# Working out the experts' order, and loading it into registers, before the first gather instead of after the first expert's first group

## The chip, the cores and the metric

The kernel runs on one core of a Trainium2 chip. A time is the device time in microseconds (us) of one execution; three were taken of the kernel before. The engines have short names in the profile: PE is TensorE (matmuls), PEld its weight loads, DVE is VectorE, ACT is ScalarE, POOL is GpSimd, SP is SyncE, which here issues nearly all transfers; SPq is SyncE's instruction queue. Each engine carries out its own list of instructions in order, and waits at an instruction until the semaphores that it names are there.

## The reference

Two layers run over 256 tokens of 1024 features (and over 256 context tokens in the first layer). The second layer ends in a mixture of 8 experts, and all that the change touches lies there: the router gives every token 8 scores, the best two count, and each expert is a gated two-layer network of width 3584.

```python
def moe_swiglu(h, router, w1, w3, w2):
    logits = (h @ router).astype(jnp.float32)
    vals, idx = lax.top_k(logits, TOP_K)          # TOP_K = 2
    wts = jax.nn.softmax(vals, axis=-1)
    combine = jnp.sum(jax.nn.one_hot(idx, N_EXPERTS) * wts[..., None], axis=-2)
    y = jnp.zeros_like(h)
    for e in range(N_EXPERTS):                    # 8 experts
        y = y + combine[..., e:e + 1] * swiglu(h, w1[e], w3[e], w2[e])
    return y
# swiglu(h, w1, w3, w2) = (silu(h @ w1) * (h @ w3)) @ w2
```

## The kernel before, in words

**Experts by rank.** An expert is not computed for all tokens. Its tokens are gathered by a matmul with a one-hot matrix into a block of 128 columns ("large") or 64 columns ("small"). Expert 0 is always large and always first. The other seven are sorted by their number of tokens while the kernel runs: the three fullest are large, the four others small. Which expert stands at which rank is known only on the chip, so SyncE loads the seven expert numbers into registers, and the address of a weight transfer is taken from a register. `SEQ` is the fixed order of the blocks: expert 0, then small and large in turn.

**The steps.** The list `steps` holds the whole kernel. A step is a function and the weight tiles that it needs; a tile is 1024 KB. An expert's 3584 hidden features are cut into seven f-groups of 512. An f-group takes six tiles: two each of `moe1` and `moe3` (the two input matrices, `eh` for large and `eh_small` for small) and two of `moe2` (the output matrix, `ey`, `ey_small`), which is computed one block later. `seq` is the list of (block, f-group): (0,0), (0,1), (1,0), (0,2), and so on, a large and a small one in turn. So the first ten tiles, those of (0,0) and (0,1) and of the output of (0,0), belong to expert 0 and have fixed addresses; the eleventh is the first of a small block and needs the registers. Here they are called tile 1 to tile 10, and tile 11 onwards.

**The path of a tile.** `issue_dma` puts the transfers on SyncE's queue in the order of the steps, as far as buffers are free: five called `raw` and five called `q`. It stops at `state["stop"]`, the first tile with an address from a register, until `order_load` lifts the stop. For a large block a tile is split: ScalarE casts it to a high part (`hi`, line 233), VectorE subtracts (`lo`, line 211), and TensorE runs three matmuls (lines 261 to 263) for each product; there are three `hi` and three `lo` buffers, and VectorE's subtraction frees the transfer's buffer. For a small block the tile is used as it came (line 1536), and the matmul frees the buffer. `ensure` writes the split of a tile into the program two tiles ahead of its step, so that the splits stand between the other instructions of ScalarE and VectorE.

**Around the change.** `route_b` chooses the two experts of each token, and sums by matmul the rank of each token within its expert (`rank`) and the number of tokens of each expert (into columns 16 to 24 of the same PSUM tile). It normalises the tokens in eight feature slices (line 1331 on VectorE, 1333 on ScalarE), transposes them into `htok` (line 1343 on TensorE), and gathers expert 0's tokens (`gather(0)`, line 1478); then it works out the weights of the two experts (`comb`) and copies the counts (`cnt`). `order_a` turns the counts into ranks (`rk`) and the expert numbers by rank (`exi`). `order_load` loads these into SyncE's registers and lifts the stop. `order_b` sorts the columns of `sel`, `comb` and `rank` by rank (`by`), and works out whether any block overflows (`cmi`, read at the very end). `onehots_small` makes the one-hots of the four small blocks, and `gather_small` gathers all four at once (line 1491 on TensorE, copied by ScalarE at line 1492). Where each is called stands in the loop at the end of the listing.

Of the kernel before, what the change touches and what calls it, by code (L numbers as in the profile page):

```python
# [22 lines left out]
F32 = mybir.dt.float32  # L23
# [8 lines left out]
P = 128  # L32
# [6 lines left out]
E = 8  # L39
# [47 lines left out]
def build(ctx, tc, io):  # L87
    nc = tc.nc
    ve, se, te = nc.vector, nc.scalar, nc.tensor
# [150 lines left out]
    def step(fn, *gs, native=False, quiet=False, late=False):  # L240


        steps.append(([(g, native) for g in gs], fn, quiet, late))
# [1053 lines left out]
    def route_b(_):  # L1297
        pb = C["ss"].bcast()
        r = C["ss"].r
        iota8 = iota[:, :E]  # L1300
        sel = cp.tile([P, 2, E], F32, name="sel")
        comb = cp.tile([P, 2, E], F32, name="comb")
        rank = cp.tile([P, 2, E], F32, name="rank")
        lgs = tiny(16).rearrange("p (t e) -> p t e", t=2)
        mx = tiny(16).rearrange("p (t e) -> p t e", t=2)
        ix = tiny(16, U32).rearrange("p (t e) -> p t e", t=2)
        for t in range(2):
            ve.scalar_tensor_tensor(lgs[:, t, :], C["lg"][t][:, :E], r[:, t:t + 1], C["c0"], op0=ALU.mult, op1=ALU.add)
            ve.max(mx[:, t, :], lgs[:, t, :])
            ve.max_index(ix[:, t, :], mx[:, t, :], lgs[:, t, :])  # L1310
        del C["lg"]
        xf = tiny(4).rearrange("p (t c) -> p t c", t=2)
        ve.tensor_copy(xf, ix[:, :, 0:2])
        o0 = tiny(16).rearrange("p (t e) -> p t e", t=2)
        o1 = tiny(16).rearrange("p (t e) -> p t e", t=2)
        for t in range(2):
            ve.tensor_scalar(o0[:, t, :], iota8, xf[:, t, 0:1], None, op0=ALU.is_equal)
            ve.tensor_scalar(o1[:, t, :], iota8, xf[:, t, 1:2], None, op0=ALU.is_equal)
        ve.tensor_add(sel, o0, o1)
        tri = cst[:, K_TRI:K_TRI + P]  # L1320
        ps = PS()
        te.matmul(ps[:, 0:E], lhsT=tri, rhs=sel[:, 0, :], start=True, stop=True)
        te.matmul(ps[:, E:2 * E], lhsT=tri, rhs=sel[:, 1, :], start=True, stop=False)
        te.matmul(ps[:, E:2 * E], lhsT=ones, rhs=sel[:, 0, :], start=False, stop=True)
        te.matmul(ps[:, 2 * E:3 * E], lhsT=ones, rhs=sel[:, 0, :], start=True, stop=False)
        te.matmul(ps[:, 2 * E:3 * E], lhsT=ones, rhs=sel[:, 1, :], start=False, stop=True)

        hn = []
        for k in range(KD):
            t = S()  # L1330
            ve.tensor_mul(t[:, :L], xt[k][:, :L], pb[:, :L])
            hn.append(xt[k][:, L:])
            se.activation(hn[k], t[:, :L], AF.Identity, bias=mod(1, SH2 + k, 0), scale=Affn[1][:, k, 0:1])
            if k == 3:
                ve.tensor_copy(rank, ps[:, 0:2 * E].rearrange("p (t e) -> p t e", t=2))
                C["sel"], C["comb"], C["rank"] = sel, comb, rank
                onehots(0)
        htok = C["htok"] = pools["t"].tile([P, 2, D], F32, tag="htok", name="htok")
        for hf in range(2):
            for t in range(2):  # L1340
                pt = PS()
                for k in range(4):
                    te.transpose(pt[:, k * P:(k + 1) * P], hn[4 * hf + k][:, t * P:(t + 1) * P], ident)
                (se.copy if t else ve.tensor_copy)(htok[:, t, hf * 512:(hf + 1) * 512], pt)
        gather(0)
        flush_tails()

        w = tiny(6).rearrange("p (c t) -> p c t", t=2)
        ve.tensor_sub(w[:, 0, :], mx[:, :, 1], mx[:, :, 0])
        se.activation(w[:, 0, :], w[:, 0, :], AF.Exp)  # L1350
        ve.tensor_scalar(w[:, 1, :], w[:, 0, :], 1.0, None, op0=ALU.add)
        ve.reciprocal(w[:, 1, :], w[:, 1, :])
        ve.tensor_mul(w[:, 2, :], w[:, 0, :], w[:, 1, :])
        for t in range(2):
            ve.tensor_scalar(o0[:, t, :], o0[:, t, :], w[:, 1, t:t + 1], None, op0=ALU.mult)
            ve.scalar_tensor_tensor(comb[:, t, :], o1[:, t, :], w[:, 2, t:t + 1], o0[:, t, :], op0=ALU.mult, op1=ALU.add)
        cnt = C["cnt"] = cp.tile([P, E], F32, name="cnt")
        ve.tensor_copy(cnt, ps[:, 2 * E:3 * E])


    SEQ = ((1, None), (0, 3), (1, 0), (0, 4), (1, 1), (0, 5), (1, 2), (0, 6))
    NR7, LARGE, SMALL = E - 1, 3, 64

    def order_a(_):

        cnt, i7 = C["cnt"], iota[:, :NR7]
        key = tiny(E)
        ve.scalar_tensor_tensor(key, cnt, float(E), iota[:, :E], op0=ALU.mult, op1=ALU.subtract)
        C["ord"] = S()[:, :4 * NR7 * NR7].rearrange("p (i c) -> p i c", i=4)
        m2 = [C["ord"][:, i, :].rearrange("p (a b) -> p a b", a=NR7) for i in range(4)]  # L1370
        k7 = key[:, 1:]
        ve.tensor_tensor(m2[0], k7.unsqueeze(1).broadcast_to([P, NR7, NR7]), k7.unsqueeze(2).broadcast_to([P, NR7, NR7]),
                         op=ALU.is_gt)
        rk = C["rk"] = cp.tile([P, NR7], F32, name="rk")
        ve.reduce_sum(rk, m2[0], axis=AX.X)
        ve.tensor_tensor(m2[1], rk.unsqueeze(1).broadcast_to([P, NR7, NR7]), i7.unsqueeze(2).broadcast_to([P, NR7, NR7]),
                         op=ALU.is_equal)
        ve.tensor_tensor(m2[2], m2[1], iota[:, 1:E].unsqueeze(1).broadcast_to([P, NR7, NR7]), op=ALU.mult)
        ex = tiny(NR7)
        ve.reduce_sum(ex, m2[2], axis=AX.X)  # L1380
        C["exi"] = cp.tile([P, NR7], I32, name="exi")
        ve.tensor_copy(C["exi"], ex)
# [21 lines left out]
        C["cmi"] = cp.tile([P, 1], I32, name="cmi")  # L1404
        ve.tensor_copy(C["cmi"], cmx)

    def order_load(_):

        _, C["ex"] = nc.values_load_multi_w_load_instructions(
            C["exi"][0:1, :], engines=[mybir.EngineType.SP], min_val=1, max_val=E - 1)  # L1410
        state["stop"] = None
        issue_dma()
# [227 lines left out]
    for i, (n, fg) in enumerate(seq):  # L1640
        prev, before = (seq[i - 1] if i else None), (seq[i - 2] if i > 1 else None)
        for part in range(2):
            if SEQ[n][0]:
                for half in range(2):
                    step(eh(n, fg, part, half), expert("moe3" if part else "moe1", n, fg, half))
            else:
                step(eh_small(n, fg, part), expert("moe1", n, fg, part), expert("moe3", n, fg, part), native=True)
            if prev and part == 0:
                step(lambda g, prev=prev: et(*prev))
        if prev:  # L1650
            for half in range(2):
                y_step(*prev, half)
        if before and before[1] == last:
            step(lambda g, m=before[0]: scatter(m))
        if i == 0:
            step(order_a)
            step(order_load)
        if i == 1:
            step(order_b)
            step(onehots_small)  # L1660
            step(gather_small)
        if fg == 3:
            step(lambda g, n=n: comb_t(n))
# [239 lines left out]
```

## Time and profile before

| | |
|---|---|
| time, median of 3 runs | 1897.54 us (1897.12 to 1899.59) |
| the profiled execution's own time | 1896.34 us |
| its span, first to last instruction | 1894.6 us |
| mean granted TensorE clock | 0.981 of 2.4 GHz |
| busy in the span: PE, DVE, ACT, POOL | 95%, 60%, 41%, 23% |
| moved by DMA | 489.99 MB, mean 259 GB/s |
| transfers of expert weights | 334 of 1024.0 KB, the last tiles in halves |

The experts' stage begins near 990 us and goes on to the end. The shares are means over stages with different limits, so the rows below come from the stretch where the change lies (980 to 1060 us), and from two stretches further on. A row with a window gives, for each engine, the busy time in us within that window; "PEclk" is the clock that was granted, and the share of the DMA engines goes up to about 1.

### The profile page before, as it was taken

The page shows a single profiled execution, that of the slowest core. Times are in us where ns is not written, and L with a number is a line of the kernel's source. Part 1 is how long each engine was busy: PE and PEld are TensorE (multiplying, and loading weights), DVE is VectorE, ACT ScalarE, POOL GpSimd, SP SyncE. Part 2 cuts the span into 40 slices and gives each one's busy share as a digit, 9 for nine tenths or more (in the row PEclk, how much of TensorE's full clock was granted, in tenths as well). Part 3 has the DMA queues.
Part 4 walks back from the last instruction along what each step waited for, and adds up shares of the span by engine and source line. Part 5 has one row for each costly group of instructions (what it writes and reads, how often), then busy time and mean ns, then how long its engine had stood idle before and what let it go on. Part 6 is the DMA issues. An engine that isn't in the chain of part 4 may idle for free.

```text
span 1894.6 us, 24116 instructions
## 1 busy us (share of the span) xinstructions
PE 1792.9 (95%) x9438; PEld 1304.5 (69%) x9438; DVE 1137.6 (60%) x1645; ACT 772.5 (41%) x867; POOL 443.5 (23%) x189
## 2 busy tenths in 40 slices
PE   6999999999999999988995999999999999999997
PEld 5889878788888888786584665656556665656563
DVE  5888873398897321768756345555555655555553
ACT  5455542522222222255634344444444444444441
POOL 1677545254444444426400000000000000000000
PEclk9999999999999999999997999999999999999999
DMA  9432153544444322420075799999999999999995
GB/s 369 161 132 90 67 199 138 197 159 175 171 159 159 119 103 89 159 108 23 21 291 222 293 419 419 417 368 410 420 420 393 399 413 420 409 376 406 419 420 213
DMA packets 71686, 489.99 MB, mean 259 GB/s; under 512 B 8080, under 2 KB 9488, under 8 KB 13200
## 3 DMA queue, kind: packets, MB, share of 16 engines
q1 hardware_dynamic: 70992, 487.88, 64.9%
q8 instruction: 76, 1.25, 0.3%
q10 hardware_dynamic: 576, 0.52, 0.1%
q14 instruction: 42, 0.34, 0.1%
HBM read 487.32 MB, written 1.05 MB: 258 GB/s over the span
## 4 chain that ended last, share of the span: by engine, by line
PE 68%; DMA 13%; DVE 11%; ACT 4%; issue 3%; SPq 0%; POOL 0%; DVEq 0%; ACTq 0%; POOLq 0%
PE p L261 17%; PE p L263 17%; PE p L262 17%; DMA raw<-in_moe 11%; PE p L1536 8%; DVE lo L211 3%; ACT hi L233 2%; PE p L1593 2%; PE p L1161 2%; DMA q<-in_moe 2%; DVE p L568 1%; PE p L1556 1%; PE p L370 1%; PE p L1143 1%; DVE s L299 1%
## 5 line engine op out<-in xcount | busy, mean ns | idle before, releaser
L211 POOL TENSOR_TENSOR lo<-raw,hi 128x2048 fp32r<-128x2048 f32 (+1 forms) x69 | 314.7, 4564 | 422.0 <-ACT hi L233 415.2
L233 ACT CAST hi<-raw 128x2048 fp32r<-128x2048 f32 x173 | 329.5, 1908 | 187.0 <-PE p L263 78.3
L261 PE MATMUL p<-s,hi 128*128 128x512 f32 x960 | 375.7, 391 | 0.7 <-ACT s L433 0.7
L262 PE MATMUL p<-s,hi 128*128 128x512 f32 x960 | 374.8, 390 | 1.5 <-DVE s L763 1.1
L263 PE MATMUL p<-s,lo 128*128 128x512 f32 x960 | 374.2, 390 | 0.6 <-POOL lo L205 0.6
L211 DVE TENSOR_TENSOR lo<-raw,hi 128x2048 fp32r<-128x2048 f32 (+1 forms) x108 | 247.0, 2289 | 87.2 <-ACT hi L233 87.2
L211 DVE TENSOR_TENSOR lo<-q,hi 128x2048 fp32r<-128x2048 f32 x69 | 158.0, 2292 | 222.0 <-ACT hi L233 222.0
L233 ACT CAST hi<-q 128x2048 fp32r<-128x2048 f32 x69 | 131.4, 1906 | 197.3 <-DMA q<-in_moe 149.7
L262 PEld LDWEIGHTS p<-s,hi 128*128 128x128 f32 x960 | 180.6, 188 | 40.2 <-DVE s L763 1.7
L261 PEld LDWEIGHTS p<-s,hi 128*128 128x128 f32 x960 | 180.7, 188 | 39.7 <-ACT s L433 0.9
L263 PEld LDWEIGHTS p<-s,lo 128*128 128x128 f32 x960 | 180.6, 188 | 38.6 <-POOL lo L205 1.1
L263 PE MATMUL p<-hi,xg 128*128 128x512 f32 x448 | 175.4, 391 | 5.4 <-DVE xg L1482 5.4
L261 PE MATMUL p<-hi,xg 128*128 128x512 f32 x448 | 179.3, 400 | 0.0
L262 PE MATMUL p<-lo,xg 128*128 128x512 f32 x448 | 175.6, 392 | 0.3 <-DVE lo L211 0.2
L262 PE MATMUL p<-lo,s 128*128 128x256 f32 (+1 forms) x480 | 161.3, 336 | 5.9 <-POOL lo L211 3.9
L261 PE MATMUL p<-hi,s 128*128 128x256 f32 (+1 forms) x480 | 164.7, 343 | 0.0
L396 DVE SCALAR_TENSOR_TENSOR s<-raw,o 128x512 f32<-128x512 f32 x128 | 158.8, 1302 | 0.0
L1536 PE MATMUL p<-q,xt 128*64 128x512 f32 x560 | 156.3, 611 | 0.0
L445 DVE SCALAR_TENSOR_TENSOR xt<-p,mod,xt 128x256 f32<-128x256 f32 x216 | 90.3, 476 | 76.9 <-PE p L263 69.5
L568 DVE SCALAR_TENSOR_TENSOR p<-s,vecs,p 128x494 f32<-128x494 f32 (+11 forms) x192 | 125.9, 736 | 6.1 <-ACT p L550 6.1
L263 PE MATMUL p<-hi,s 128*128 128x512 f32 (+1 forms) x352 | 123.6, 351 | 0.0
L261 PEld LDWEIGHTS p<-hi,s 128*128 128x128 f32 x480 | 92.4, 192 | 30.2 <-issue 21.9
(252 smaller groups left out, 2225.0 us busy)
## 6 DMA issues: line engine op xcount, KB each, us to landing
raw<-in_moe SPq DMA_DIRECT2D x181, 1024.0 KB, 10.3
q<-in_moe SPq DMA_DIRECT2D x153, 1024.0 KB, 13.9
raw<-in_ff SPq DMA_DIRECT2D x42, 1024.0 KB, 4.8
raw<-in_ada SPq DMA_DIRECT2D x31, 1024.0 KB, 5.8
raw<-in_adaT SPq DMA_DIRECT2D x16, 1024.0 KB, 4.9
raw<-in_w_ag SPq DMA_DIRECT2D x8, 1024.0 KB, 6.9
raw<-in_w_uv SPq DMA_DIRECT2D x8, 1024.0 KB, 4.9
raw<-in_w_out SPq DMA_DIRECT2D x6, 1024.0 KB, 5.0
```

Source lines behind the costliest of these rows:

```text
L211: eng.tensor_sub(lo[:, sl], r[:, sl], f32(hi[:, sl]))
L233: se.copy(hi, raws[i])
L261: te.matmul(out, lhsT=lh[0], rhs=rh[0], start=first, stop=False, skip_group_check=True)
L262: te.matmul(out, lhsT=lh[0], rhs=rh[1], start=False, stop=False, skip_group_check=True)
L263: te.matmul(out, lhsT=lh[1], rhs=rh[0], start=False, stop=last, skip_group_check=True)
L299: ve.tensor_add(self.acc[:, :n], self.acc[:, :n], q[:, :n])
L396: ve.scalar_tensor_tensor(j, g[0][:, jj * D + q * 512:jj * D + (q + 1) * 512], 1.0, C["cb"][s][q], op0=ALU.mult, op1=ALU.mult, accum_out=h ...
L445: ve.scalar_tensor_tensor(xt[d][:, sl], ps[:, sl], mod(l, gbase + d, s), xt[d][:, sl], op0=ALU.mult, op1=ALU.add)
L568: ve.scalar_tensor_tensor(ov[:, :, lo:hi], gv[:, :, lo + s:hi + s], vecs[:, w0 + j:w0 + j + 1], ov[:, :, lo:hi], op0=ALU.mult, op1=ALU.add)
L1161: te.matmul(ps[HD * z:HD * z + HD, :L], lhsT=v, rhs=t[:, z, c, :], start=(c == 0), stop=(c == 3), skip_group_check=True, tile_position=(0, ...
L1536: te.matmul(ps[SMALL * z:SMALL * (z + 1), :], lhsT=xt[k][:, o:o + SMALL], rhs=w[z][:, kk, :], start=(k == 0), stop=(k == 7), skip_group_ch ...
L1593: te.matmul(yps[n][SMALL * z:SMALL * (z + 1), :], lhsT=hT[:, f * SMALL:(f + 1) * SMALL], rhs=w[:, ff, z * 512:(z + 1) * 512], start=(fg == ...
```

## The change

Four things are moved; nothing is computed anew and nothing is left out.

- The copy of the counts, `order_a` and `order_load` go from behind the first block's step into `route_b`, between the fourth and the fifth of the eight feature slices, right behind the one-hots of expert 0. They are called there directly and are no steps any more.
- `order_b` goes from behind the second block's last step to a step behind the first half of (0,0).
- `onehots_small` goes from the same place to a step behind the second half of (0,0).
- `gather_small` stays where it was.

```diff
@@ route_b
                 C["sel"], C["comb"], C["rank"] = sel, comb, rank
                 onehots(0)
+                cnt = C["cnt"] = cp.tile([P, E], F32, name="cnt")
+                ve.tensor_copy(cnt, ps[:, 2 * E:3 * E])
+                order_a()
+                order_load()
...
-        cnt = C["cnt"] = cp.tile([P, E], F32, name="cnt")
-        ve.tensor_copy(cnt, ps[:, 2 * E:3 * E])
...
-    def order_a(_):
+    def order_a():
...
-    def order_load(_):
+    def order_load():
@@ the loop over seq
             if prev and part == 0:
                 step(lambda g, prev=prev: et(*prev))
+            if i == 0:
+                step(onehots_small if part else order_b)
...
-        if i == 0:
-            step(order_a)
-            step(order_load)
         if i == 1:
-            step(order_b)
-            step(onehots_small)
             step(gather_small)
```

In the rows of the program's order a line number, an operation, the output and the inputs stand in a row, and a number behind a name tells buffers apart. On VectorE, in `route_b`, this stood behind the one-hots of expert 0 (lines 1331 and 1344 are the normalised slices and the copies of the transposed tokens):

```order
L1426 TENSOR_SCALAR s_8232<-cst,rank,sel 128x128 x2
L1331 TENSOR_TENSOR s_8235<-xt_84,p_8190 128x256
L1331 TENSOR_TENSOR s_8238<-xt_85,p_8190 128x256
L1331 TENSOR_TENSOR s_8241<-xt_86,p_8190 128x256
L1331 TENSOR_TENSOR s_8244<-xt_87,p_8190 128x256
L1344 COPY htok<-p_8248 128x512
```

and this stands there now, where the lines after the change are two or four higher:

```order
L1428 TENSOR_SCALAR s_8232<-cst,rank,sel 128x128 x2
L1339 COPY cnt<-p_8213 128x8
L1370 SCALAR_TENSOR_TENSOR t_8237<-cnt,cst 128x8
L1374 TENSOR_TENSOR s_8239<-t_8237 128x49
L1377 TENSOR_REDUCE rk<-s_8239 128x7
L1378 TENSOR_TENSOR s_8239<-rk,cst 128x49
L1380 TENSOR_TENSOR s_8239<-s_8239,cst 128x49
L1382 TENSOR_REDUCE t_8245<-s_8239 128x7
L1384 CAST exi<-t_8245 128x7
L1331 TENSOR_TENSOR s_8317<-xt_84,p_8190 128x256
```

Eight small instructions now stand ahead of the fifth slice. Further on in VectorE's list, the small blocks' one-hots (line 1436) stood behind the subtractions of tiles 15, 16 and 17 (`q_8467` to `q_8471`) and behind `order_b`, whose last row is `cmi`:

```order
L211 TENSOR_TENSOR lo_8554<-q_8467,hi_8553 128x2048
L211 TENSOR_TENSOR lo_8572<-q_8469,hi_8571 128x2048
L211 TENSOR_TENSOR lo_8588<-q_8471,hi_8587 128x2048
L1392 TENSOR_TENSOR s_8385<-s_8385,sel 128x49
L1393 TENSOR_REDUCE by_8591<-s_8385 128x7
...
L1405 CAST cmi<-t_8612 128x1
L1436 TENSOR_SCALAR s_8617<-cst,by_8601,by_8591 128x64 x8
```

and now they stand among the subtractions of expert 0's own tiles (`q_7819` is tile 5, `raw_7884` tile 6, `raw_7952` tile 7, `raw_8103` tile 8), with `order_b` ahead of tile 6:

```order
L211 TENSOR_TENSOR lo_8428<-q_7819,hi_8427 128x2048
L1394 TENSOR_TENSOR s_8239<-s_8239,sel 128x49
...
L1407 CAST cmi<-t_8454 128x1
L211 TENSOR_TENSOR lo_8473<-raw_7884,hi_8472 128x2048
L1523 TENSOR_TENSOR s_8490<-s_8490,p_8459 128x512
L211 TENSOR_TENSOR lo_8494<-raw_7952,hi_8493 128x2048
L1438 TENSOR_SCALAR s_8499<-cst,by_8443,by_8433 128x64 x8
L211 TENSOR_TENSOR lo_8522<-raw_8103,hi_8521 128x2048
```

`order_b`'s 19 instructions moved ahead of eight subtractions (tiles 6 to 10 and 15 to 17), the one-hots ahead of six. On SyncE's queue, the register load and what stood behind it (tile 11 is the first DMA):

```order
L185 DMA raw_8170<-in_moe 128x2048
L1409 TENSOR_LOAD exi
L1409 ISA x14
L185 ISA
L185 DMA raw_8459<-in_moe 128x2048
L185 ISA
L185 DMA raw_8461<-in_moe 128x2048
L185 ISA
L185 DMA q_8463<-in_moe 128x2048
```

and now:

```order
L185 DMA raw_8170<-in_moe 128x2048
L1411 TENSOR_LOAD exi
L1411 ISA x14
L185 ISA
L185 DMA q_8313<-in_moe 128x2048
L185 ISA
L185 DMA q_8315<-in_moe 128x2048
L185 ISA
L185 DMA q_8394<-in_moe 128x2048
```

The queue's order is the same; the buffers differ. Tiles 11 and 12 now take the two `q` buffers that are free in `route_b`; tiles 13, 14 and 15 take the `q` buffers of tiles 3, 4 and 5, and tiles 16 to 20 the `raw` buffers of tiles 6 to 10, each as that tile's subtraction ends.

## Rows read from the trace of the kernel before

**Rows 1.** Busy time in stretches of 10 us; columns in the first line.

```profile
core 0: us, PE busy (x) PEld busy (x) DVE busy (x) ACT busy (x) POOL busy (x), PEclk, DMA share, GB/s
1010.00:1020.00 10.00, 9.39 (x41) 7.12 (x39) 6.94 (x5) 2.58 (x3) 0.00 (x0) 1.00 0.64 251
1020.00:1030.00 10.00, 0.00 (x0) 0.00 (x0) 0.68 (x1) 2.01 (x2) 0.00 (x0) 0.62 1.02 429
...
1040.00:1050.00 10.00, 8.45 (x28) 7.09 (x29) 1.72 (x8) 2.23 (x6) 0.00 (x0) 0.68 0.00 0
1050.00:1060.00 10.00, 10.00 (x46) 4.17 (x46) 1.18 (x2) 1.92 (x4) 0.00 (x0) 1.00 0.41 152
```

**Rows 2.** Timeline of TensorE around its gap: start, duration, line, operation, idle before.

```profile
1019.24 0.39 PE L263 MATMUL p<-hi,s 128*128 128x512 f32 x1
1041.55 9.50 PE L1491 MATMUL p<-s,htok 128*128 128x256 f32 x32 [21.93 <-DVE s L1436]
1050.99 3.65 PE L1536 MATMUL p<-raw,xt 128*64 128x512 f32 x16
```

**Rows 3.** Waits of SyncE's queue: total us, times, longest us.

```profile
SPq L1409 <- DVE exi L1382: 33.2, 1, 33.2
```

**Rows 4.** Timeline of SyncE's queue, the first transfers behind the register load.

```profile
1012.40 0.95 SPq L185 DMA_DIRECT2D raw<-in_moe  x2
```

**Rows 5.** Chain of work that ended last, 950 to 1070 us: start, duration, what.

```profile
1015.61 16.68 DMA q<-in_moe
```

**Rows 6.** Timeline of VectorE, from 982 us to the small blocks' one-hots.

```profile
982.43 1.41 DVE L1331 TENSOR_TENSOR s<-xt,p 128x256 f32<-128x256 f32 x4
...
993.95 0.16 DVE L1358 COPY cnt<-p 128x8 f32<-128x8 f32 x1
994.45 6.70 DVE L211 TENSOR_TENSOR lo<-q,hi 128x2048 fp32r<-128x2048 f32 x3 [0.35 <-ACT hi L233]
1001.57 2.29 DVE L211 TENSOR_TENSOR lo<-raw,hi 128x2048 fp32r<-128x2048 f32 x1 [0.42 <-ACT hi L233]
...
1005.28 2.29 DVE L211 TENSOR_TENSOR lo<-raw,hi 128x2048 fp32r<-128x2048 f32 x1 [0.82 <-ACT hi L233]
1007.49 0.16 DVE L1368 SCALAR_TENSOR_TENSOR t<-cnt,cst 128x8 f32<-128x8 f32 x1
...
1008.97 0.17 DVE L1382 CAST exi<-t 128x7 int32<-128x7 f32 x1
1009.05 4.49 DVE L211 TENSOR_TENSOR lo<-raw,hi 128x2048 fp32r<-128x2048 f32 x2
...
1014.06 2.28 DVE L211 TENSOR_TENSOR lo<-raw,hi 128x2048 fp32r<-128x2048 f32 x1
...
1036.52 0.20 DVE L1392 TENSOR_TENSOR s<-s,sel 128x49 f32<-128x49 f32 x1
...
1039.79 0.15 DVE L1405 CAST cmi<-t 128x1 int32<-128x1 f32 x1
1039.86 1.87 DVE L1436 TENSOR_SCALAR s<-cst,by,by 128x64 f32<-128x64 f32 x8
```

**Rows 7.** Timeline of ScalarE: the last of three casts, and the gather's first copy.

```profile
1032.38 1.90 ACT L233 CAST hi<-q 128x2048 fp32r<-128x2048 f32 x1 [0.60 <-DMA q<-in_moe]
1043.66 0.37 ACT L1492 COPY xt<-p 128x256 f32<-128x256 f32 x1 [9.38 <-PE p L1491]
```

**Rows 8.** Busy time and granted clock in stretches of 2 us.

```profile
982.00:984.00 2.00, 1.96 (x8) 1.32 (x7) 2.00 (x7) 1.85 (x5) 0.00 (x0) 0.50 0.15 53
...
988.00:990.00 2.00, 2.00 (x19) 2.00 (x18) 0.24 (x1) 0.58 (x1) 0.00 (x0) 0.93 0.00 0
...
1046.00:1048.00 2.00, 2.00 (x10) 1.78 (x9) 0.00 (x0) 0.73 (x2) 0.00 (x0) 0.92 0.00 0
```

**Rows 9.** Busy time in two stretches of 25 us, later.

```profile
1185.00:1210.00 25.00, 23.88 (x110) 13.59 (x109) 13.68 (x9) 9.85 (x9) 0.00 (x0) 1.00 1.01 419
1210.00:1235.00 25.00, 23.19 (x114) 17.16 (x112) 15.58 (x11) 14.52 (x12) 0.00 (x0) 0.93 0.90 366
```


## The prediction

> **What bounds the kernel now.** I read the busy shares over the span first. TensorE leads nearly everywhere and has two dips; the one inside the experts' stage, near 1030 us, lies where the change is. Windows of 10 us over that stretch [rows 1] show what the reader should see: from 1020 to 1030 us TensorE does nothing while the DMA engines are full, and from 1040 to 1050 us it is the other way round. One waits for the other in turn, where they should overlap. The timeline of TensorE gives the size [rows 2]: the last matmul of the first output group starts at 1019.24 and is done at 1019.5 (41 matmuls in 9.39 us, 0.229 each [rows 1]); the small blocks' gather starts at 1041.55, after 21.93 us of idle, released by VectorE's one-hots.
>
> Then I followed the wait backwards. The one-hots stand in VectorE's list behind `order_b` and the subtractions of tiles 15 to 17. Those waited for ScalarE's casts, the casts for transfers, and the chain shows the transfer (16.68 us from 1015.61 [rows 5]). The transfers could not start before SyncE had its registers: its queue stood 33.2 us at the register load, waiting for `exi` [rows 3]. `exi` is written at 1008.97 to 1009.14 [rows 6], and the first transfer behind the load is issued at 1012.40 [rows 4], 3.26 us later. SyncE was ready from 976 us on (33.2 before 1009.2). So a line of small VectorE instructions, placed late, holds back every weight transfer, and TensorE pays at the end of the line.
>
> Once the stage runs, the DMA engines are the bound: share 1.01 at 419 GB/s from 1185 to 1210 us, with TensorE busy for 23.88 of 25 us [rows 9]. A tile of 1.049 MB takes 1.049 / 0.419 = 2.50 us there. From 1210 us, where an expert changes, the share falls to 0.90, and the transfers wait for buffers for a while. The two are close to each other all the way, so time won at the start must be won by both.
>
> **The change, part by part.** All times are those of the profiled execution.
>
> *In front of the first gather.* `order_a` takes 1009.14 - 1007.49 = 1.65 us, the counts 0.16 and a pause, together 1.85 us [rows 6]. They now stand ahead of the second four slices, which began at 982.43 and feed ScalarE, then TensorE's transposes, then the gather and the first matmul. Nothing hides them, as each follows the one before at once: cost 1.85 us. TensorE's clock is at its half rate here (0.50 from 982 us, 0.93 between 988 and 990 us [rows 8], so up to 988.3, 6.3 us), and the new pause falls in the middle: TensorE starts again near 985.2, when the fifth slice has come through VectorE (0.35) and ScalarE (estimated at the same). If the full rate comes at the same time, nothing is added; if it comes 6.3 us after the second start, at 991.5, half rate lasts 3.2 us more, which costs half of that, 1.6 us. I take 0.8, bounds 0 and 1.6.
>
> The Trainium skill, "TensorE: Matmul & The Clock Gate", Part 1, says that an idle array falls to half its clock and only sustained activity releases it; this trace agrees (0.62 and 0.68 in the windows around the 21.93 us gap [rows 1]). It speaks against putting work in front of TensorE at this place, and by it the cost is nearer 1.6 than 0.
>
> *The transfers.* `exi` is now done at 982.43 + 1.85 = 984.3, and the first issue follows 3.26 us later, at 987.5 instead of 1012.40. Only this load stood at the head of the queue; what is behind it is transfers, and nobody else uses the queue. Tiles 11 and 12 find free buffers. Tiles 13 to 20 take the buffers of tiles 3 to 10 as their subtractions end, in the trace between 996.7 and 1016.3 [rows 6], so one by one they land by about 1025. They run beside matmuls, as they already did at 1013 to 1019 us with TensorE at 9.39 of 10 [rows 1]; I cost that at nothing.
>
> *VectorE in the first f-groups.* `order_b` takes 1039.86 - 1036.52 = 3.34 us and the one-hots 1.87 [rows 6]; both now stand between the subtractions of expert 0's tiles, and `order_a`'s 1.65 leaves. Without the shift from above: tile 5's subtraction ends at 1001.15 (994.45 + 6.70), `order_b` at 1004.5, tile 6 at 1006.75 (before 1003.86), the product of the first hidden group (0.6, the gap up to the row at 1005.28 less its idle 0.82) at 1007.4, tile 7 at 1009.65 (before 1007.57), the one-hots at 1011.5, tiles 8 and 9 at 1016.0, the split of the hidden values (0.6, the gap ahead of 1014.06) at 1016.6, and tile 10 at 1018.9 (before 1014.06 + 2.28 = 1016.34). VectorE is then busy without a pause and TensorE waits for it: tile 10 is 2.5 us late. If TensorE's pauses absorb more it is 1.5; if nothing is absorbed it is 3.34 + 1.87 - 1.65 = 3.56. I take 2.5.
>
> *The gap.* TensorE ends the output group at 1019.5 + 1.85 + 0.8 + 2.5 = 1024.6. The one-hots are there by then. ScalarE still has the casts of tiles 15 to 17 ahead of the gather's copies; the last needs the buffer that tile 10's matmuls free, and takes 1.90 us [rows 7]. The gather writes ahead into other PSUM banks meanwhile, so this is hidden; without that cover it would cost about 2 us. The gather took 9.50 us with the clock at half rate up to about 1046.3 (0.92 in the window from 1046 [rows 8]): 4.75 us at half rate, so 2.4 us less at the full rate, 7.1 us. It ends at 1031.7, and the first half of the small block, 3.65 us [rows 2], at 1035.3. Before, that was 1050.99 + 3.65 = 1054.6. TensorE is 19.3 us ahead.
>
> *What is late next.* The eleventh tile behind the load restarted the transfers at about 1055.9 (share 0.41 of the window [rows 1]), 1.3 us after that half. Now that tile needs only tile 15's subtraction; the next, tile 22, needs the half: 1036.6 instead of 1055.9 + 2.5 = 1058.4, so 21.8 us ahead. From there the program is the same, with ten full buffers in both cases. The end is therefore between 19.3 and 21.8 us earlier; as the DMA engines bound the stage that follows, and TensorE is close, I take 20.5. 1896.34 - 20.5 = 1875.8. The profiled execution lies 1.2 under the median of the runs, 1897.54, so the forecast is 1877.0.
>
> **The rivals.** A measurement of this kernel tells about 0.2% (4 us) from no change.
>
> *VectorE's queue costs more.* The 5.2 us in the first f-groups are not absorbed at all, casts that wait for late matmuls lengthen the chain again, and 2.5 becomes 5.2. For it: VectorE is the only engine without a pause there. Against: subtraction and matmul of a tile are about equally long. 1877.0 + 2.7 = 1879.7.
>
> *The transfers do not come forward*, because a buffer or the queue holds them as before. The one-hots are still early, but ScalarE's casts of tiles 15 to 17 end near 1034.3 [rows 7] ahead of the gather's copies, so the small block's first half ends at about 1034.3 + 4 copies of 0.37 [rows 7] + 3.65 = 1039.4. That is 15.2 us ahead: 1882.3. Against: SyncE's wait names `exi` alone, and two buffers are free.
>
> *The lead is given back*, where the transfers wait for buffers anyway (share 0.90 from 1210 us [rows 9]) and the other distribution of `raw` and `q` buffers waits longer: half is lost, 1887. Against: a stretch in which all engines start earlier and do the same ends earlier.
>
> *The clock stays down* in the first f-groups: the pause ahead of the gather keeps TensorE at 1.2 GHz through the ten tiles, 120 matmuls of 0.229 us, which then take 27.5 us more, and hide VectorE's delay. TensorE ends at 1019.5 + 1.85 + 27.5 = 1048.9, later than the gather began before; the small half ends at 1048.9 + 7.1 + 3.65 = 1059.6 instead of 1054.6, and the time is about 1902.5. It decides from the point where half rate lasts 41 us longer than now, since half of that is the gain. Against: after the start at 1041.55 the clock was back within 4.75 us.
>
> **How the numbers follow.** Forecast 0.78, VectorE 0.10, transfers held 0.05, lead given back 0.04, clock 0.03. The forecast's own range is from 1874.0 (clock 0, VectorE 1.5, the transfers' lead counts: 21.8 + 0.8 + 1.0 = 23.6 saved) to 1880.1 (clock 1.6, VectorE 3.56, TensorE's lead counts: 19.3 - 0.8 - 1.1 = 17.4). I widen it to 1871, as tile 21 is even further ahead, and to 1884, which takes in the first two rivals. Faster by over 0.2%: 0.78 + 0.10 + 0.05 and most of 0.04, so 0.95. Slower: 0.03. The rest, 0.02, is no change.
>
> **What would show it.** Right: the register load near 984 us and transfers from 988 us; VectorE busy without a pause from 996 to 1021 us; no gap of more than 3 us ahead of the gather, which runs at 1024 to 1032 us with the clock at 1.00; transfers without a break from about 1037 us; the last transfer and the end some 20 us earlier. Wrong: TensorE idle ahead of the gather by more than that; a break of the transfers after 1037 us; the clock at 0.50 beyond 992 us; a lead at 1060 us that is smaller at the end.

## The result, and the profile after

| | before | changed |
|---|---|---|
| median of the runs | 1898.57 us (4 runs, 1897.12 to 1902.24) | 1879.4 us (3 runs, 1877.55 to 1880.8) |
| ratio, with its 95% interval | | 0.9893 [0.9876, 0.991] |
| profiled execution | 1896.34 us | 1877.55 us |
| its span | 1894.6 us | 1875.8 us |

The forecast was 1877.0 us, in a range of 1871 to 1884. A fourth execution of the changed kernel took 3115.7 us at a mean granted clock of 0.66 and is left out (with it the median is 1880.1), as is one of 2558.2 us at 0.65 of the experiment with the ranks behind the slices. The ratio times 1897.54, the median that the forecast started from, is 1877.2 us: a gain of 20.3 us, 17.1 to 23.5 by the interval, where 20.5 were forecast. By the two medians the gain is 19.2 us.

To compare two traces I need an instruction that stands ahead of everything that moved. I take the routing's last broadcast matmul, L320, and call its start the landmark. In the kernel before, TensorE's timeline (start, duration, line, operation, idle before and what ended it) has it here:

```profile
977.70 0.70 PE L320 MATMUL p<-s,ones 128*128 128x256 f32 x2 [0.87 <-DVE s L315]
```

The same timeline of the changed kernel, from the landmark to the first half of the small block:

```profile
979.99 0.70 PE L320 MATMUL p<-s,ones 128*128 128x256 f32 x2 [0.87 <-DVE s L315]
...
988.65 2.80 PE L1347 MATMUL p<-ident,xt 128*128 128x128 f32 x8 [1.91 <-ACT xt L1333]
...
1011.55 0.50 PE L262 MATMUL p<-lo,xg 128*128 128x512 f32 x1 [1.50 <-DVE lo L211]
...
1018.34 0.50 PE L262 MATMUL p<-lo,xg 128*128 128x512 f32 x1 [0.56 <-DVE lo L211]
...
1026.20 0.39 PE L263 MATMUL p<-hi,s 128*128 128x512 f32 x1
1026.43 7.07 PE L1493 MATMUL p<-s,htok 128*128 128x256 f32 x32
1033.43 3.65 PE L1538 MATMUL p<-q,xt 128*64 128x512 f32 x16
```

The landmark itself came 2.29 us later (979.99 for 977.70), although nothing in front of it had changed; the same program again had it at 983.62. The gap of 21.93 us [rows 2] is gone. TensorE waits twice, 1.50 and 0.56 us, for VectorE's `lo`; the last matmul of the output group starts at 1026.20, the gather follows without a wait, and the first half of the small block starts at 1033.43. From the landmark that is 53.44 us, and before it was 1050.99 - 977.70 = 73.29: a lead of 19.85 us. The profiled times then add up: 19.85 less the 2.29 of the landmark, and 1.2 that the rest won (from that half to the end 843.6 us before, 842.4 after), are the 18.8 us between the spans.

The busy times in stretches of 10 us, columns in the first line, show the two engines beside each other, where they took turns before [rows 1]:

```profile
core 0: us, PE busy (x) PEld busy (x) DVE busy (x) ACT busy (x) POOL busy (x), PEclk, DMA share, GB/s
1010.00:1020.00 10.00, 7.93 (x36) 6.22 (x36) 10.00 (x13) 6.63 (x6) 0.00 (x0) 1.00 0.78 278
1020.00:1030.00 10.00, 10.00 (x46) 8.43 (x46) 9.72 (x7) 6.66 (x6) 0.00 (x0) 1.00 0.98 392
1030.00:1040.00 10.00, 10.00 (x49) 5.12 (x49) 1.55 (x2) 2.45 (x6) 0.00 (x0) 1.00 0.22 69
1040.00:1050.00 10.00, 10.00 (x45) 7.46 (x42) 4.08 (x3) 4.75 (x4) 0.00 (x0) 1.00 1.01 421
```

From 1020 to 1030 us TensorE is busy for all of its 10 us and the DMA engines are at 0.98. The transfers then rest once, from about 1030 to 1038 us (0.22), which I read as full buffers, and run at 1.01 afterwards.

SyncE's queue: first its waits (total us, times, longest), then its timeline of issues.

```profile
SPq L1411 <- DVE s L1331: 10.4, 1, 10.4
```

```profile
990.89 15.43 SPq L185 DMA_DIRECT2D q<-in_moe  x5
...
1026.12 11.34 SPq L185 DMA_DIRECT2D q<-in_moe  x2
```

The wait at the register load is 10.4 us instead of 33.2 [rows 3], and the first transfer is issued at 990.89 instead of 1012.40 [rows 4]. It is put down to VectorE's L1331, the instruction next to `exi`, which is written at 987.64; from there to the issue it is 3.25 us, as before (3.26). The transfers follow as buffers come free; the two issues from 1026.12 on stretch over 11.34 us, which is the rest seen above. In the chain of work that ended last (start, duration, what) the longest transfer of this stretch is now 5.45 us, where 16.68 stood before [rows 5]:

```profile
1003.77 5.45 DMA q<-in_moe
```


VectorE's timeline has the moved work in its new places:

```profile
982.50 1.41 DVE L1331 TENSOR_TENSOR s<-xt,p 128x256 f32<-128x256 f32 x4
...
985.71 0.16 DVE L1339 COPY cnt<-p 128x8 f32<-128x8 f32 x1
...
987.47 0.17 DVE L1384 CAST exi<-t 128x7 int32<-128x7 f32 x1
987.54 1.40 DVE L1331 TENSOR_TENSOR s<-xt,p 128x256 f32<-128x256 f32 x4
...
999.25 6.70 DVE L211 TENSOR_TENSOR lo<-q,hi 128x2048 fp32r<-128x2048 f32 x3 [0.43 <-ACT hi L233]
1005.86 0.20 DVE L1394 TENSOR_TENSOR s<-s,sel 128x49 f32<-128x49 f32 x1
...
1009.12 0.15 DVE L1407 CAST cmi<-t 128x1 int32<-128x1 f32 x1
...
1014.21 1.87 DVE L1438 TENSOR_SCALAR s<-cst,by,by 128x64 f32<-128x64 f32 x8
1016.00 4.49 DVE L211 TENSOR_TENSOR lo<-raw,hi 128x2048 fp32r<-128x2048 f32 x2
...
1021.00 2.28 DVE L211 TENSOR_TENSOR lo<-raw,hi 128x2048 fp32r<-128x2048 f32 x1
```

Counts and ranks stand from 985.71 to 987.64 between the two halves of the four slices, `order_b` from 1005.86 to 1009.27 behind tile 5's subtraction, and the one-hots 1014.21 to 1016.08 ahead of tile 8's. From 999.25 on there is no pause, and tile 10's subtraction (1021.00) is done at 1023.28 [rows 6]. ScalarE's casts of tiles 15 to 17 go ahead of the gather's first copy; the row shows the last of them:

```profile
1026.63 1.91 ACT L233 CAST hi<-raw 128x2048 fp32r<-128x2048 f32 x1 [0.80 <-PE p L263]
1028.43 1.16 ACT L1494 COPY xt<-p 128x256 f32<-128x256 f32 x3
```

The copies start at 1028.43, 2 us after the gather, which runs on into other banks; it takes 7.07 us instead of 9.50. TensorE's clock is why. These windows (columns as above, the clock is the third number from the end) answer to [rows 8]:

```profile
990.00:992.00 2.00, 1.99 (x10) 1.88 (x10) 0.69 (x1) 1.05 (x3) 0.00 (x0) 0.50 0.10 16
992.00:994.00 2.00, 2.00 (x17) 2.00 (x17) 0.00 (x0) 0.13 (x2) 0.00 (x0) 0.82 0.80 299
1026.00:1028.00 2.00, 2.00 (x11) 1.74 (x10) 2.00 (x2) 1.37 (x1) 0.00 (x0) 1.00 1.08 385
```

The granted clock goes from 0.50 to 1.00 between 992 and 994 us and is 1.00 in every window from there to 1065 us, as TensorE no longer idles ahead of the gather: at 1026 us it is at 2.4 GHz, where before it had fallen to 1.2. Later the stage is as it was: the two windows of [rows 9] are now

```profile
1185.00:1210.00 25.00, 23.13 (x119) 17.15 (x120) 13.36 (x11) 11.51 (x11) 0.00 (x0) 1.00 1.01 418
1210.00:1235.00 25.00, 25.00 (x119) 14.87 (x118) 15.40 (x16) 10.23 (x8) 0.00 (x0) 1.00 0.84 332
```

with the DMA engines again at 1.01 and 418 GB/s until an expert changes.

### The profile page after: what moved, and what is told of

Same layout as the page of the kernel before. It is cut to its first block, busy times and chain, and to the rows that moved or that the text cites. A ratio compares the mean times of both kernels' runs of the same rounds, so it can differ in the third digit from the quotient of the medians.

```text
span 1875.8 us, 24122 instructions
## 1 busy us (share of the span) xinstructions
PE 1790.5 (95%) x9438; PEld 1303.1 (69%) x9438; DVE 1136.1 (61%) x1645; ACT 772.5 (41%) x867; POOL 444.3 (24%) x189
## 4 chain that ended last, share of the span: by engine, by line
PE 70%; DMA 12%; DVE 10%; ACT 4%; issue 3%; SPq 0%; POOL 0%; DVEq 0%; ACTq 0%; POOLq 0%
PE p L261 17%; PE p L263 17%; PE p L262 17%; DMA raw<-in_moe 8%; PE p L1538 8%; DVE lo L211 3%; DMA q<-in_moe 3%; ACT hi L233 2%; PE p L1595 2%; PE p L1161 2%; DVE p L568 1%; PE p L1558 1%; PE p L370 1%; PE p L1143 1%; DVE s L1523 1%
## 5 line engine op out<-in xcount | busy, mean ns | idle before, releaser
L1538 PE MATMUL p<-q,xt 128*64 128x512 f32 x552 | 150.3, 602 | 0.0
## 6 DMA issues: line engine op xcount, KB each, us to landing
raw<-in_moe SPq DMA_DIRECT2D x181, 1024.0 KB, 10.2
```

Of the source, the lines that this page charges most:

```text
L1538: te.matmul(ps[SMALL * z:SMALL * (z + 1), :], lhsT=xt[k][:, o:o + SMALL], rhs=w[z][:, kk, :], start=(k == 0), stop=(k == 7), skip_group_ch ...
```

## Experiments

All ratios are to runs of the kernel before on the same chip. "Lead" is the start of the small block's first half after the landmark, against the 73.29 us of before.

**The changed kernel again.** No edit.

> The changed kernel once more, as the yardstick for the others on the same chip. Both theories: 1877 to 1881 us, 0.989 of the kernel before. In the profile of the changed kernel TensorE stood 2.3 us later than before already ahead of the first instruction that the change moves (977.70 before, 979.99 after, first broadcast matmul of the routing, line 320). If that is chance, it differs here; if the change causes it, it is 2.3 us here too.

Measured: 1879.19 us (1873.13 to 1883.23), ratio 0.989 [0.9867, 0.9912], lead 19.8. The result repeats; one run can lie 4 to 6 us from the median. The landmark stands at 983.62 us here, so its shift comes with the execution, not with the change.

**Only the early load.** The sums by rank and the one-hots go back to their old place:

```diff
-            if i == 0:
-                step(onehots_small if part else order_b)
...
+            step(order_b)
+            step(onehots_small)
             step(gather_small)
```

> Only the first half of the change: ranks and register load ahead of the first gather, but the sums by rank and the small one-hots at their old place, behind the subtractions of tiles 15 to 17. Theory (the gap was a chain of two links: late transfers, then one-hots queued behind splits): transfers start as early as in the changed kernel, tile 10 is 2.5 us earlier than there, but the one-hots wait for the third cast (buffer free near 1024, cast and subtraction to 1028.5), 3.3 us of sums and 1.9 of one-hots: gather near 1033.6 instead of 1026.4, an idle of 8 to 10 us on TensorE, clock down again; 1888 us, 10 less than before. Rival A (only the transfers mattered): 1877, as good as or better than the full change. Rival B (only VectorE's order mattered): 1897 to 1899, no gain.

Measured: 1889.15 us, ratio 0.9948 [0.9929, 0.9966], lead 11.1 us. SyncE's queue and TensorE:

```profile
988.66 15.41 SPq L185 DMA_DIRECT2D q<-in_moe  x5
```

```profile
1030.99 9.05 PE L1493 MATMUL p<-s,htok 128*128 128x256 f32 x32 [9.30 <-DVE s L1438]
1039.97 3.65 PE L1538 MATMUL p<-q,xt 128*64 128x512 f32 x16
```

The transfers come as early as in the changed kernel, and that alone brings half of it. But the one-hots stand behind the subtractions of the next tiles, and TensorE idles 9.30 us. The gather then takes 9.05 us, for 7.07 in the changed kernel, as the clock has fallen again (0.50 from 1025 to 1030 us).

**Only the early sums and one-hots, first try.** The conversion to `exi` and the load stand behind tile 7's subtraction. The number was kept in a persistent tile of its own for this, 28 bytes for each partition.

```diff
-                order_load()
...
-        C["exi"] = cp.tile([P, NR7], I32, name="exi")
-        ve.tensor_copy(C["exi"], ex)
+        ex = C["exf"] = cp.tile([P, NR7], F32, name="exf")
...
             if i == 0:
+                if part:
+                    step(lambda g: order_load())
```

> Only the second half: ranks, sums by rank and one-hots stand where the change put them, but the conversion to integers and with it the register load wait until behind the subtraction of tile 7, near 1014.3 us in the changed kernel's time (its load was at 987.6). Theory: the one-hots are early, the transfers start near 1018.7, tile 17 lands 17 to 18 us later, and the gather's copies on ScalarE stand behind its cast: first copy near 1039, the small block's first half ends near 1045 instead of 1037.1; 1887 us, 11 to 12 less than before. Rival A (only the transfers mattered): 1897 to 1902. Rival B (only VectorE's order mattered): 1879 to 1880, the full gain.

Measured: 1897.59 us, ratio 0.999 [0.9978, 1.0003]. It does not tell what it should. Its landmark, ahead of all that was moved, is already 16 us later than the changed kernel's:

```profile
996.41 0.70 PE L320 MATMUL p<-s,ones 128*128 128x256 f32 x2 [0.87 <-DVE s L315]
```

From there the lead is 9.7 us. The added tile had changed something else, which the last experiment takes up.

**Counts and ranks twice, first try.** `order_a` is called twice in front, and the second call got persistent tiles of its own (`rk` and `exi`).

```diff
+                order_a()
                 order_a()
                 order_load()
```

> The changed kernel with the seven instructions of the ranks carried out twice in front of the second four slices: 1.65 us more on VectorE at the place where the prediction said that nothing hides it. Theory: 1.7 to 2.5 us longer than the changed kernel, some of it through the clock staying at 1.2 GHz for longer; the pause of TensorE in the transposes grows from 1.9 to 3.6 us. Rival (the place is covered by transposes and gather): no difference, within 0.5 us.

Measured: 1893.2 us, ratio 0.9971 [0.9954, 0.9988]. The same thing spoils it: the landmark stands at 993.91 us, and the lead from there is 18.9 us, so the second `order_a` itself cost about 1.

**Only the early sums and one-hots, in the same memory.** The sums are written into `exi`'s own tile and converted in place, late.

```diff
-                order_load()
...
-        ex = tiny(NR7)
-        ve.reduce_sum(ex, m2[2], axis=AX.X)
-        ve.tensor_copy(C["exi"], ex)
+        ve.reduce_sum(C["exi"].bitcast(F32), m2[2], axis=AX.X)
...
     def order_load():
+        ve.tensor_copy(C["exi"], C["exi"].bitcast(F32))
```

> The second half of the change alone once more (register load behind tile 7's subtraction, one-hots early), now with the expert numbers converted in place, so that every tile lies in memory where the changed kernel has it. The earlier form had one persistent tile of 28 bytes more, and its TensorE was already 16 us late ahead of the first moved instruction. Theory: 1886 to 1889 us, the small block's first half starts about 63.6 us after the broadcast matmul of the routing (53.4 in the changed kernel, 73.3 before). Rival A (only the transfers mattered): 1897 to 1902. Rival B (only VectorE's order mattered): 1879 to 1880.

Measured: 1888.24 us, ratio 0.9949 [0.9928, 0.997], landmark 978.53, lead 9.7. The first transfers behind the load, and the gather:

```profile
1016.30 0.95 SPq L185 DMA_DIRECT2D raw<-in_moe  x2
```

```profile
1025.16 5.34 PE L1491 MATMUL p<-s,htok 128*128 128x256 f32 x24
1038.39 3.78 PE L1491 MATMUL p<-s,htok 128*128 128x256 f32 x8 [7.89 <-ACT xt L1492]
1042.10 4.58 PE L1536 MATMUL p<-raw,xt 128*64 128x512 f32 x16
```

The first of these is issued 37.77 us after the landmark, 3.1 later than before (1012.40 - 977.70): the first expert matmul comes 2.6 us later here (15.62 us after the landmark, for 13.06), and `order_b` stands ahead of the load. The one-hots are early, and 24 of the gather's 32 matmuls run at once. Then TensorE waits 7.89 us for ScalarE, whose copies stand behind casts that wait for the late transfers. So each half of the change wins about 10 us, and each leaves a different wait in the same gap; the leads of 11.1 and 9.7 add up to 20.8, about the 19.85 of both.

**Counts and ranks twice, in the same memory.** As above, the second call writing the same tiles.

```diff
+                order_a()
                 order_a()
...
-        rk = C["rk"] = cp.tile([P, NR7], F32, name="rk")
+        rk = C["rk"] = C.get("rk") or cp.tile([P, NR7], F32, name="rk")
...
-        C["exi"] = cp.tile([P, NR7], I32, name="exi")
+        C["exi"] = C.get("exi") or cp.tile([P, NR7], I32, name="exi")
```

> The ranks twice in front of the second four slices once more, both times into the same tiles, so that nothing else lies elsewhere in memory. Theory: the pause in the transposes grows from 1.9 to 3.6 us, and the small block's first half starts 1.5 to 2.5 us later after the routing's broadcast matmul than the 53.4 us of the changed kernel; 1880.5 to 1882. Rival (covered): 53.4 us and 1879.

Measured: 1878.98 us, ratio 0.9906 [0.9885, 0.9926]; the time can't be told from the changed kernel's. On TensorE (one of five pairs of count matmuls, and the second four slices):

```profile
980.31 0.37 PE L1323 MATMUL p<-sel,cst 128*128 128x8 f32 x2
...
986.54 2.80 PE L1348 MATMUL p<-ident,xt 128*128 128x128 f32 x8 [2.70 <-ACT xt L1333]
```

The pause grows from 1.91 to 2.70 us and the lead shrinks by 0.84, less than the 1.5 to 2.5 expected. The count matmuls ran at full rate here (0.37 us a pair, for 0.57 in the changed kernel) and were done about 1 us sooner, which hides some of it. The version before this one also counted at full rate, and had 1.56 us of VectorE between the slices for 3.33 here. Against it the second eight transposes start 1.77 us later after the landmark (9.12 for 7.35), but the first expert matmul only 0.80 (16.42 for 15.62), as `gather(0)` takes 4.84 us here for 5.81 there. So what stands in front is paid for, but by less than half: the pause falls into time at half rate.

**Counts, ranks and load behind the second four slices.** The four calls move from between the slices to ahead of `gather(0)`.

```diff
-                cnt = C["cnt"] = cp.tile([P, E], F32, name="cnt")
-                ve.tensor_copy(cnt, ps[:, 2 * E:3 * E])
-                order_a()
-                order_load()
...
+        cnt = C["cnt"] = cp.tile([P, E], F32, name="cnt")
+        ve.tensor_copy(cnt, ps[:, 2 * E:3 * E])
+        order_a()
+        order_load()
         gather(0)
```

> The changed kernel with counts, ranks and register load put behind the copies of the transposed tokens, where VectorE stood idle for 3.2 us waiting for the gather, still ahead of the gather in the program. Theory: the ranks are hidden there, TensorE's pause of 1.9 us in the transposes goes, the load is 3 to 4 us later than in the changed kernel, which the transfers can afford as tiles 13 to 20 wait for buffers anyway: 1.9 to 3.5 us less than the changed kernel, 1876 to 1878. Rival (the early transfers set the time): 3 to 4 us more than the changed kernel.

Measured: 1878.88 us (5 runs, 1874.27 to 1886.22), ratio 0.9881 [0.9861, 0.9901], lead 20.8. TensorE, and the window in which its clock comes back:

```profile
984.67 4.82 PE L1343 MATMUL p<-ident,xt 128*128 128x128 f32 x16
989.28 5.35 PE L1480 MATMUL p<-s,htok 128*128 128x128 f32 x32
```

```profile
992.00:994.00 2.00, 2.00 (x17) 2.00 (x16) 0.50 (x1) 0.58 (x1) 0.00 (x0) 0.84 0.00 0
```

The pause is gone, and all 16 transposes run in one piece. But of the 1.9 us expected at least, 0.95 arrive. The clock comes back when it did in the changed kernel: some 12.8 us after the landmark here, 12.7 there (estimated from this window's 0.84 and the other's 0.82). So the 1.91 us of the pause are now filled with work at half rate, which is worth half, and `gather(0)` takes 5.35 us, for 4.45 in the changed kernel. The later waits for `lo` stay (2.0 us).

**Part of the sums later.** The sums of `comb` and the overflow count, 11 of `order_b`'s 19 instructions, move behind the small gather, as nobody needs them before.

```diff
-        for a in (C["sel"], C["comb"], C["rank"]):
+        for w in (0, 2):
+            a = (C["sel"], C["comb"], C["rank"])[w]
...
             step(gather_small)
+            step(order_c)
```

> The changed kernel with 11 of the 19 instructions of the sums by rank (those of the weights, and of the overflow check) moved behind the small gather: 2.0 us less on VectorE between the subtractions of tiles 5 and 6. Theory: VectorE was without a pause there and TensorE waited 1.5 and 0.6 us for its subtractions; both waits shrink to 0.3 or less, 1.5 to 2 us less than the changed kernel, 1877.5 to 1878. Rival (the stage behind is bound by transfers alone, and these wait for the small block's first half in any case): the wait goes, but the time does not, within 0.5 us.

Measured: 1878.92 us, ratio 0.9879 [0.986, 0.9898]. TensorE's waits for `lo` fall from 2.1 to 0.4 us and the lead grows by 1.86 to 21.7. In the time it can't be told from the changed kernel, so its rival, that the stage behind takes the gain back, is not excluded.

**Both of the last two.**

> Both of the last two edits together. Theory: the gains add up, 3.5 to 5 us less than the changed kernel, 1874 to 1876, about 0.987 of the kernel before. Rival (one limit behind both): no better than the better of the two.

Measured: 1872.19 us (1871.45 to 1877.12), ratio 0.9853 [0.9834, 0.9872], the fastest kernel of this case and below the 1874 expected. Its interval lies under that of the changed kernel's first comparison and overlaps that of its second a little. TensorE:

```profile
1014.41 0.50 PE L262 MATMUL p<-lo,xg 128*128 128x512 f32 x1 [0.43 <-DVE lo L211]
...
1022.52 7.07 PE L1504 MATMUL p<-s,htok 128*128 128x256 f32 x32
1029.52 3.65 PE L1549 MATMUL p<-q,xt 128*64 128x512 f32 x16
```

The lead is 22.7 us, 2.85 more than the changed kernel's, the sum of the two parts (0.95 + 1.86). The median is some 7 us lower. The other 4 are not shown by the trace; executions of one kernel differ by as much.

**One tile more.** To explain the two spoiled runs: the changed kernel with one more persistent tile that nobody reads.

```diff
         ve.memset(ones, 1.0)
+        ve.memset(cp.tile([P, 7], F32, name="pad"), 0.0)
```

> The changed kernel with one unused persistent tile of 28 bytes more, written once at the start; every tile behind it lies 32 bytes higher. It measures by itself what the first forms of the last two experiments had besides their edits. Theory (the place of the tiles in memory makes the matmuls of the first half slower): 1893 to 1897 us, matmuls of the feed-forward stage at a pace of 0.233 us instead of 0.227, routing reached some 16 us later. Rival (it was the edits): 1879.

Measured: 1889.42 us (1888.08 to 1892.26), ratio 0.9956 [0.9942, 0.997], less of a loss than the 1893 to 1897 expected. Busy times of a stretch of 50 us well before the change, first of the changed kernel, then of this one, and this one's landmark:

```profile
500.00:550.00 50.00, 50.00 (x223) 41.39 (x222) 39.42 (x76) 13.04 (x11) 20.32 (x6) 1.00 0.46 166
```

```profile
500.00:550.00 50.00, 50.00 (x216) 40.27 (x215) 34.10 (x62) 10.59 (x9) 23.69 (x5) 1.00 0.37 131
```

```profile
992.61 0.70 PE L320 MATMUL p<-s,ones 128*128 128x256 f32 x2 [0.87 <-DVE s L315]
```

TensorE is busy for all of both stretches, at a clock of 1.00, with 223 matmuls in one and 216 in the other. The landmark is 12.6 us later, and from there the lead is as before (small block at 1046.16, so 53.55). The unused tile costs about 10 us of the time, far from where the change is, and both spoiled runs show the same 216 matmuls.

## Why the prediction was right

**What bounds.** Right: a late line of small VectorE instructions held back transfers and one-hots. The two half versions show it from both sides: with the early load alone 9.30 us of the gap remain, and with the early one-hots alone 7.89.

**In front of the first gather.** Right in the sum, wrong in its parts. Counts and ranks: 1.85 forecast, 1.93 measured on VectorE. With 0.8 for the clock, 2.65 us were forecast for the first expert matmul; it starts 995.56 - 979.99 = 15.57 us after the landmark, for 990.76 - 977.70 = 13.06 before, so 2.5. I had counted the 1.85 in full, as nothing hides them. But the version with the ranks behind the slices, which is without the pause, gets only 0.95 of it back. It still starts its first expert matmul 1.57 us later than before (14.63 after the landmark), with nothing of the change ahead of its transposes or its gather. Those 1.57 are the clock, which the two windows show, first of the kernel before, then of the changed one:

```profile
980.00:982.00 2.00, 1.65 (x12) 1.52 (x12) 1.84 (x8) 1.34 (x3) 0.00 (x0) 0.86 0.98 414
```

```profile
982.00:984.00 2.00, 1.36 (x7) 1.36 (x7) 1.87 (x8) 1.05 (x3) 0.00 (x0) 0.62 1.01 426
```

With the windows of [rows 8] and those above I estimate half rate from 981.4 to 988.3 us before and from 982.5 to 992.7 in the changed kernel, 10.2 us for 6.8. Half of the 3.4 more is 1.7, where I took 0.8 (0 to 1.6). The version without the pause has 10.2 us as well, so here it isn't the pause that kept the clock down; what did is open, as there is one trace of the kernel before. So a delay that cost half of what I took and a clock that cost twice as much nearly cancel, and 2.5 beside 2.65 is luck. By the trace's own clock half rate goes on past 992 us, which I had named as a sign of being wrong; 2.29 us of that are the late landmark. The warning that I drew from the Trainium skill, "TensorE: Matmul & The Clock Gate", Part 1, that the cost is nearer 1.6, came true in size, but not through the pause: the version without it pays the same.

**The transfers.** The first issue was forecast for 987.5 us; 990.89 less the 2.29 of the landmark is 988.6. None of the casts of tiles 15 to 17 waited for a transfer any more; the last waited 0.80 us for TensorE.

**The first f-groups.** 2.5 forecast (1.5 to 3.56). TensorE's waits are 1.50 + 0.56 = 2.06, and tile 10's subtraction is 4.65 us later against the landmark, 2.15 of it here. The experiment with part of the sums later takes 1.86 of them away, so they were on the path.

**The gap.** The output group was forecast to end 5.15 us later than before, and was 4.67 later against the landmark. The gather: 7.1 forecast, 7.07 measured, nothing idle in front of it. The casts ahead of the copies were hidden, as costed.

**The lead and what is late next.** 19.3 forecast at the small block, 19.85 measured. From there to the end it was 842.4 us, for 843.6 before; over the versions with the same memory this stretch takes 842.2 to 852.0, so one pair of profiles can't show it closer than that. The rival of the lead given back was put at 1887 and falls with the medians, 1879.4 and 1879.2. The rival of a clock that stays down fell with the windows at 1.00. The rival of a costlier VectorE queue, 1879.7, can't be told from the forecast by the time; it falls with the waits, 2.06 us where it had 5.2. The total of 20.5 stands beside 19.2 to 20.3, with an interval of 17.1 to 23.5: the mechanism is shown, the closeness is luck.

**What was priced wrongly.** The rival in which the transfers don't come forward was put at 15.2 us of gain; its experiment had a lead of 9.7. There the small block starts 63.57 us after the landmark, where that rival had 1039.4 - 3.65 - 977.70 = 58.05. Of the 5.5 between them, 2.9 are the load, which comes that much later than the rival had it; the casts end at 1038.06. The other 2.6 stand behind the casts: I had put four copies there, 1.45 us, but TensorE still owes eight of the gather's matmuls, and these 4.04 us end at 1042.10. The forecast didn't rest on it.

**What I did not allow for** is the scatter ahead of the change: 2.29 us at the landmark in the profiled execution, and 977.4 to 983.6 over the profiles of kernels with the same memory. It lies within the range, and a difference of 2 or 3 us in this kernel can be told only from the trace.

## What to carry to other kernels

When two engines wait for each other in turn, follow both waits back: here one late queue entry held the transfers and another the one-hots, and removing only one would have left some 8 to 9 us of the gap. Small instructions that decide a DMA's address belong in front of large ones, even on the path: in the version with the early load alone, 2.5 us of delay at the first expert matmul bought a lead of 11.1. A pause costs less than its length where the work that it displaces runs at half rate: 0.95 of 1.91 us here. Count small gains from a landmark ahead of the edit, and keep the list of tiles in memory the same between versions, or the comparison measures that too.

## What the hardware did that I had not expected

**One more tile in memory slows TensorE's pace.** In the kernel before and in all versions with its memory, matmuls of 128x512 follow each other at 0.227 us (222 or 223 records in the 50 us from 500 us on, and 1026.20 to 1026.43 above). With a further tile of 28 bytes it is 216 records, and by the starts in the timeline 0.233 us, at the same granted clock of 1.00. Two versions had one such tile more and the third had two, and all three show it. It does not touch all products: in the last experiment's trace the products of `hi` and `lo` with an `s` tile go at 0.233 us in the experts' stage too, those with `xg` at 0.227. That the place of the two operands in memory is the cause is likely and was not isolated.

**Short waits, and a clock that dips.** In the experts' stage, with the DMA engines at a share of 1.01 for most of it, TensorE's clock dips in two to seven places of five profiles. In the version with the ranks behind the slices, two windows and the line of TensorE's timeline at the dip are

```profile
1090.00:1100.00 10.00, 7.10 (x26) 2.40 (x24) 8.59 (x7) 4.88 (x4) 0.00 (x0) 0.75 1.01 418
1100.00:1110.00 10.00, 10.00 (x42) 6.61 (x39) 2.88 (x2) 3.92 (x3) 0.00 (x0) 0.91 1.01 419
```

```profile
1095.60 1.11 PE L1558 MATMUL p<-ident,s 128*128 128x128 f32 x4 [2.90 <-DVE s L1523]
```

A wait of 2.90 us, and the granted clock is 0.75 in that window and 0.91 in the next. In most such windows TensorE is idle for 1.5 to 3 us. The time not granted (window times one less its clock, summed over 1070 to 1870 us) goes, in these five profiles, with the length of the stage from the small block to the end: 3.4 us of it and 842.4 in the changed kernel, 5.1 and 843.6 before, 5.1 and 844.4 in the changed kernel's repeat, 11.9 and 849.0 with the early load alone, 11.9 and 852.0 in the version shown. That is some 8 us between executions that do the same work there, more than most edits above are worth. The four other profiles with the same memory have 5.8 to 6.9 us and 842.2 to 845.8, not in strict order, and that the dips cause the length is not shown. What decides how many of the waits bring the clock down stays open too.

**A count that lands on either rate.** The ten count matmuls ahead of the change run at 0.37 us a pair or at 0.57, in executions of kernels that are the same up to there; the changed kernel's profile had the slow kind, the kernel before the fast one, and some change over between two pairs. The granted clock falls ahead of them or behind them: the windows of 2 us in which it falls are 0.86 before and 0.62 in the changed kernel, as shown above. Of the 1.57 us of the clock this is 1.0: the transposes start 4.80 us after the landmark in both versions with slow counts compared above, for 3.82 before.
